# Two-layer decoder trunk: the pool of the shared tiles begins 128 bytes further on, and a rotation's scratch moves into spare columns

## The chip, the core and the metric

The kernel runs on one core of one Trainium2 chip. The metric is the device time of one execution in microseconds (us), the median of three runs. Everything is float32, or float32 split into two float32r parts, so that TensorE multiplies at its fast rate and the result keeps more digits.

## What is computed

The reference is a decoder trunk of two layers over 1024 positions of width 1024:

```python
mem_n = rmsnorm(mem, mem_norm_g)
for i in range(2):
    hn = rmsnorm(x, attn_norm_g[i])
    mix, q_cross = mla_mixer(...) if i % 2 == 0 else swa_mixer(...)
    cross = memory_cross_attention(q_cross, mem_n, w_mem_kv[i])
    x = x + concat([mix, cross]) @ w_o[i]
    a = relu(rmsnorm(x, mlp_norm_g[i]) @ w_up[i])
    x = x + (a * a) @ w_down[i]
return rmsnorm(x, final_norm_g)
```

Layer 0 mixes with latent attention of 12 heads (a low-rank projection of 928 columns: 384 for queries, 256 for keys and values, 32 for one rotary key shared by the heads, 256 for cross-attention queries). Layer 1 mixes with a sliding window of 128. In both, 4 heads attend to a memory of 256 positions. The MLP is 1024 to 4096 and back.

## The kernel before, in words

**Split products.** A product of two float32 matrices is three matmuls: high x high, high x low, low x high. `split` (L99, L100) makes the parts: ScalarE copies the value into float32r, VectorE subtracts. `mm3` (L108 to L110) and `mm3w` (L117 to L120) issue the triples, as do the up projection (L1402 to L1404) and the down projection (L1705 to L1707). Most matmuls are 128x128 weights by 512 columns.

**Stages.** Memory projections for both layers (to 36 us in the trace); layer 0's input projection (`a_in`, 43 to 141 us); its value, cross-attention, key and query work (to 245 us); the twelve heads (to 453 us); the output projection (`wo_phase`, to 558 us); the MLP's up phase (`mlp`, 558 to 873 us) and down phase (`Down`, to 1184 us). Then layer 1: input projection (`feat_mm`, to 1347 us), window attention (to 1429 us), output projection (to 1523 us), up (to 1837 us), down (to 2151 us).

**The up and down projections** use Strassen's scheme: seven products of half-size blocks in place of eight. In the up phase each of the seven right operands X[1] to X[7] stays in SBUF. X[1] and X[2] lie in the shared tiles q0 and q1, X[6] and X[5] in f0 and f1 (`open_x`, `wo_phase`); X[3], X[4] and X[7] lie in tiles of the right-hand pools. They are the moving operands, and the weights (128 columns of w_up or of sums of its blocks) come from right-hand tiles. Each product of one block of weights is twelve matmuls: four tiles of depth by the three terms. There are 16 blocks in a layer. In the down phase both operands of nearly all matmuls are right-hand tiles; the last eight steps of layer 1 take their moving operand from q0 and q1.

**Pools and addresses.** SBUF is filled from two sides. On the left side stand, in this order, `const` (constants, masks, gains, sine and cosine, `padl`), `quad`, and above it whatever the stage needs: `pa` (layer 0's input weights), `kvp` (values), `hb` (heads 0, 3, 6, 9), later `kv1p`, `qcp`, `q1p`. On the right side stand `padr` and the pools `xq`, `pm`, `cp`, `wu`, `hb1` (the other heads), `at`, `xnp`, `ws`, `rest`, `ores`. `quad` holds the large shared tiles: f0, f1, q0, q1 of 16 KB a partition each and two raw tiles of 4 KB, which change their use from stage to stage. In the profile they appear under the names of their uses: fa, fb, wm, xhls, qc, kq, woq, xnh, wf, mqf (f0 and f1 in the MLP), mqq (q0 and q1 in the MLP), wor, wsr, mr.

In the built kernel `const` begins at byte 16512 of a partition and ends at 19456, which is 76 x 256. So `quad` begins on a multiple of 256 bytes, and so do its tiles, their rows of 2 KB, and the tiles of `pa`, `kvp`, `hb`, `kv1p`, `qcp` and `q1p`. The right-hand pools `rest`, `ws`, `xnp`, `hb1`, `cp` and `wu` begin 128 bytes past a multiple of 256, `pm` 192 bytes past one. A row of `pa` is 3712 bytes, so its slices alternate between a multiple of 256 and 128 past one.

**The rotation.** `rope` (L298) rotates a row of heads: four VectorE products (L307 to L310), two of them into scratch tiles a and b, then a subtraction and an addition on POOL (L311, L312). It is called for one head of 32 columns in `a_in` (L619, eight times, scratch 64 bytes each with two buffers, from `pa`) and for twelve heads in `q_rope` (eight times, scratch from `wu2`). `a_in` writes its result to f1[:, t % 2, 0:928]; columns 928 to 1023 of those rows are not used then.

**Order.** The order of instructions on each engine follows the program text, with a scheduler of the tile framework that may move neighbouring work where it sees an engine waiting. DMAs of the large tiles go through SP's queue.

Of the kernel before, what the change touches and what calls it, by code (L numbers as in the profile page):

```python
# [9 lines left out]
F32 = mybir.dt.float32  # L10
# [9 lines left out]
P = 128  # L20
# [10 lines left out]
MLA_IN = 928  # L31
# [24 lines left out]
def trunk(  # L56
# [12 lines left out]
    def pool(name, side="left", space=None, bufs=1):  # L69
        kw = {"reuse_waits": "tile"}  # L70
        if space is not None:
            kw["space"] = space
        return tc.alloc_tile_pool(name=name, bufs=bufs, side=side, **kw)

    const = pool("const")
# [3 lines left out]
    def ps2(name):  # L79
        return psum[0].tile([P, 1024], F32, tag="s", bufs=2, name=name)  # L80
# [31 lines left out]
    def mm3w(pss, terms):  # L112

        n = len(terms)
        for i, (ah, al, bs) in enumerate(terms):
            for ps, (bh, bl) in zip(pss, bs):
                nc.tensor.matmul(ps, ah, bh, start=i == 0, stop=False)  # L117
                nc.tensor.matmul(ps, ah, bl, start=False, stop=False)
            for ps, (bh, bl) in zip(pss, bs):
                nc.tensor.matmul(ps, al, bh, start=False, stop=i == n - 1)  # L120
# [51 lines left out]
    def rstd_of(pl, src_parts, junk):  # L172

        k = len(src_parts)
        small_ct[0] += 1
        ss = pl.tile([P, 2], F32, tag="ss", bufs=4, name=f"ss{small_ct[0]}")
        z = pl.tile([P, 2], F32, tag="zs", bufs=4, name=f"zs{small_ct[0]}")
        for i, (ap, n) in enumerate(src_parts):
            nc.scalar.activation(junk[:, :n], ap, AF.Square, accum_out=ss[:, i : i + 1])
            nc.vector.tensor_scalar(z[:, i : i + 1], ss[:, i : i + 1], 1.0 / n, EPS, ALU.mult, ALU.add)  # L180
        return newton(pl, ss, z[:, :k], k)
# [38 lines left out]
    cosb = const.tile([P, NT, 16], F32, name="cosb")  # L220
    sinb = const.tile([P, NT, 16], F32, name="sinb")

    padl = const.tile([P, 16], F32, name="padl")
    padr_p = pool("padr", "right")
    padr = padr_p.tile([P, 24], F32, name="padr")
    nc.gpsimd.memset(padl, 0.0)
# [68 lines left out]

    rope_ct = [0]

    def rope(pl, src, dst, t, nh):  # L298

        rope_ct[0] += 1  # L300
        c = cosb[:, t : t + 1, :].to_broadcast([P, nh, 16])
        s = sinb[:, t : t + 1, :].to_broadcast([P, nh, 16])
        a = pl.tile([P, nh, 16], F32, tag="ra", bufs=2, name=f"ra{rope_ct[0]}")
        b = pl.tile([P, nh, 16], F32, tag="rb", bufs=2, name=f"rb{rope_ct[0]}")
        x1, x2 = src[:, :, 0:16], src[:, :, 16:32]
        V = nc.vector
        V.tensor_tensor(dst[:, :, 0:16], x1, c, ALU.mult)  # L307
        V.tensor_tensor(a, x2, s, ALU.mult)
        V.tensor_tensor(dst[:, :, 16:32], x1, s, ALU.mult)
        V.tensor_tensor(b, x2, c, ALU.mult)  # L310
        nc.gpsimd.tensor_tensor(dst[:, :, 0:16], dst[:, :, 0:16], a, ALU.subtract)  # L311
        nc.gpsimd.tensor_tensor(dst[:, :, 16:32], dst[:, :, 16:32], b, ALU.add)  # L312
# [179 lines left out]
    def quad_tile(tag, name, dt=F32):  # L492
        return quad.tile([P, 4, S], dt, tag=tag, bufs=1, name=name)
# [4 lines left out]
    fa0, f1 = quad_tile("f0", "fa0"), quad_tile("f1", "fa1")  # L498
# [26 lines left out]
    pa = pool("pa")  # L525
# [82 lines left out]
    CQC, CKR = 640, 896  # L608
    def a_in(t):
        xh, xl = xT.pop(t)  # L610
        ps = ps2(f"psin{t}")
        mm3w([ps[:, 0:512], ps[:, 512:MLA_IN]],
             [(xh[:, kt, :], xl[:, kt, :], [(wih[:, kt, 0:512], wil[:, kt, 0:512]), (wih[:, kt, 512:MLA_IN], wil[:, kt, 512:MLA_IN])]) for kt in range(KT)])
        c = f1[:, t % 2, 0:MLA_IN]
        rs = rstd_of(pa, [(ps[:, 0:QR], QR), (ps[:, QR : QR + KVR], KVR)], c)
        nc.vector.tensor_scalar(c[:, 0:QR], ps[:, 0:QR], rs[:, 0:1], None, ALU.mult)
        nc.vector.tensor_scalar(c[:, QR : QR + KVR], ps[:, QR : QR + KVR], rs[:, 1:2], None, ALU.mult)
        nc.scalar.activation(c[:, CQC : CQC + 256], ps[:, 672:928], AF.Copy, scale=0.125)
        rope(pa, ps[:, 640:672].rearrange("p (h c) -> p h c", h=1), c[:, CKR : CKR + 32].rearrange("p (h c) -> p h c", h=1), t, 1)  # L619
        cs_[t] = c  # L620

    def a_cT(t):
# [13 lines left out]
    for k in range(NT + 2):  # L636
        if 0 < k < NT:
            a_T(k)
        if 0 < k < NT - 1:
            a_N(k + 1)  # L640
        if 1 <= k <= NT:
            a_in(k - 1)
        if 3 <= k <= NT:
            next(loading, None)
        if 2 <= k <= NT:
            a_cT(k - 2)
# [157 lines left out]
    for j in range(6):  # L804
# [4 lines left out]
        ps = ps2(f"pskn{j}")  # L809
# [18 lines left out]
    def q_rope(t):  # L828
        sl = slice(t * P, (t + 1) * P)
        pq = ps1(f"psqr{t}")[:, 0:384]  # L830
        mm3(pq, [(cTh[:, kt, sl], cTl[:, kt, sl], *wqr[kt]) for kt in range(3)])
        qts[t] = f1[:, (t // 2) % 2, (t % 2) * 512 : (t % 2) * 512 + 384]
        rope(wu2, pq.rearrange("p (h c) -> p h c", h=H), qts[t].rearrange("p (h c) -> p h c", h=H), t, H)
# [100 lines left out]
    def values(h, G, k, late):  # L934

        vh, vl = vbufs[h % 2]
        c0 = 512 - width(G, k)
        order = [b[1] for b in blocks_of(h) if b[0] == G]
        first, last = k == order[0], k == order[-1]
        mms = []  # L940

        def mm(o, a, b, **kw):
            mms.append(lambda: nc.tensor.matmul(o, a, b, skip_group_check=True, **kw))  # L943

        if first and not late:
            po_[(h, G)] = ps1(f"pso{h}_{G}")
        po = po_[(h, G)]
        if (G, k) in WHOLE:
            if late:
                return [], lambda: None  # L950
            mm(po[:, c0:], vfs[h % 2][:, k, :], probs.pop((h, G, k))[:, c0:], start=first, stop=last)
        elif late:
            mm(po[:, c0:], vh[:, k, :], probs.pop((h, G, k, "late"))[:, c0:], start=False, stop=last)
        else:
            ph, probs[(h, G, k, "late")] = probs.pop((h, G, k))
            mm(po[:, c0:], vh[:, k, :], ph[:, c0:], start=first, stop=False)
            mm(po[0:64, c0:], vl[:, k, :], ph[:, c0:], start=False, stop=False)
            last = False

        def then():  # L960
            if not last:
                return
            r = slice((h % 2) * 64, (h % 2) * 64 + 64)
            if h == H - 1:
                if G:
                    last_o(G, at.tile([64, 512], F32, tag="on", bufs=2, name="rq1"))
                return
            on = at.tile([65, 512], F32, tag="on", bufs=2, name=f"on{h}_{G}")
            nc.scalar.activation(on, po[0:65], AF.Copy)
            nc.sync.dma_start(out=qn[h // 2][r, G * 512 : (G + 1) * 512], in_=on[0:64])  # L970
            c = [c for c in range(3) if h >= GRP[c]][-1]
            d0 = (h - GRP[c]) * NT + 4 * G
            nc.sync.dma_start(out=den[c][d0 : d0 + 4, :], in_=on[64:65])

        return mms, then
# [59 lines left out]
    for n in range(len(seq) + LB):  # L1035
# [3 lines left out]
        for lag, late in ((LB, True), (LV, False)):  # L1039
            if 0 <= n - lag < len(seq):  # L1040
                a, b = values(*seq[n - lag], late)
# [16 lines left out]
        h, j = divmod(n, NB)  # L1058
# [788 lines left out]
    f1 = quad_tile("f1", "fb1")  # L1847
# [230 lines left out]
```

## Time and profile before

| | |
|---|---|
| median of 3 runs | 2145.2 us (2143.55 to 2147.43) |
| profiled execution, first to last instruction | 2151.4 us, 28963 instructions |
| mean granted TensorE clock | 0.994 |
| longest single wait of TensorE (at the end of the heads) | 5.6 us |
| DMA | 286.84 MB, mean 133 GB/s |
| HBM | 183.01 MB read, 76.85 MB written |

The page gives no time for the profiled execution other than its span. In the rows of the profile, `out<-in` names the written tile and then the read ones without their buffer numbers; for a matmul the first after the arrow is the moving operand, the second the weights. "x112 | 44.2, 395 | 0.0" are count, total busy us, mean ns of one, and idle us of the engine just before. A matmul's duration is longer than the step from one to the next, since they are pipelined; the end is modelled.

### The profile page before, as it was taken

To read this page: it belongs to the slowest core of one execution; us is meant where nothing else is said; L and a number is where in the kernel's file an instruction comes from. 1 tells how busy PE (TensorE), PEld (TensorE's weight loads), DVE (VectorE), ACT (ScalarE), POOL (GpSimd) and SP (SyncE) were. 2 spreads that over 40 slices of the span, in tenths; PEclk is the share of its full clock that TensorE was granted. 3 is DMA by queue.
4 is the path that set the end of the run, shared out by engine and by line. 5 is a ranking of instruction groups with operands and counts; after the bars stand their busy time and mean duration, and the time that the engine had idled before them with its cause. 6 is when DMAs were issued, how large, how long until landed. Compare 5 with 4: busy or idle time off the path is not lost.

```text
span 2151.4 us, 28963 instructions
## 1 busy us (share of the span) xinstructions
PE 2113.6 (98%) x9830; PEld 1697.7 (79%) x9830; DVE 1473.3 (68%) x2915; ACT 1106.6 (51%) x2406; POOL 148.9 (7%) x251
## 2 busy tenths in 40 slices
PE   7999999989999999999999999999999999999998
PEld 6888766668888788888888878668888888788886
DVE  7767677764987677886557632776987766876665
ACT  6555466655754543444445432866844453444453
POOL 1001001010000000000001121530000000000000
PEclk9999999999999999999999999999999999999999
DMA  6202223333354445954433534132354446954432
GB/s 225 84 1 71 54 67 92 94 114 103 103 174 144 138 162 190 326 179 147 146 115 108 152 79 118 40 128 84 103 181 142 140 149 212 321 167 142 133 119 87
DMA packets 176436, 286.84 MB, mean 133 GB/s; under 512 B 16627, under 2 KB 68448, under 8 KB 176288
## 3 DMA queue, kind: packets, MB, share of 16 engines
q1 hardware_dynamic: 169648, 266.30, 39.1%
q0 software_dynamic: 5328, 16.07, 2.1%
q10 hardware_dynamic: 1312, 2.63, 0.4%
q8 instruction: 77, 1.26, 0.2%
q14 instruction: 71, 0.58, 0.1%
HBM read 183.01 MB, written 76.85 MB: 121 GB/s over the span
## 4 chain that ended last, share of the span: by engine, by line
PE 90%; DVE 4%; DMA 3%; ACT 2%; issue 1%; POOL 0%; SPq 0%; DVEq 0%; ACTq 0%; POOLq 0%
PE psy L1705 5%; PE psy L1707 5%; PE psy L1706 5%; PE psu L1402 5%; PE psu L1404 5%; PE psu L1403 5%; PE psz L1705 4%; PE psz L1707 4%; PE psz L1706 4%; PE psv L1404 4%; PE psv L1403 4%; PE psv L1402 4%; PE pso L943 3%; PE pss L913 3%; PE pswo L110 3%; PE pswo L108 3%
## 5 line engine op out<-in xcount | busy, mean ns | idle before, releaser
L1302 ACT ACTIVATE mr<-mr,gcol 128x256 f32<-128x256 f32 (+1 forms) x160 | 67.6, 477 | 79.4 <-DMA mr<-in_mlp_w_up_dram 70.4
L923 ACT ACTIVATE p<-pss 128x512 f32<-128x512 f32 (+2 forms) x144 | 68.4, 486 | 69.3 <-DVE pss L921 52.4
L1705 PE MATMUL psy<-g 128*128 128x512 f32 x256 | 99.9, 390 | 0.0
L1706 PE MATMUL psy<-g 128*128 128x512 f32 x256 | 99.6, 389 | 0.0
L1707 PE MATMUL psy<-g 128*128 128x512 f32 x256 | 99.4, 390 | 0.0
L99 ACT ACTIVATE g<-i 128x512 fp32r<-128x512 f32 x79 | 49.7, 629 | 93.5 <-PE psz L1706 46.3
L1302 ACT ACTIVATE d<-d,gcol 128x256 f32<-128x256 f32 x128 | 57.6, 500 | 75.2 <-DMA d<-in_mlp_w_up_dram 61.4
L100 DVE TENSOR_TENSOR g<-i,g 128x512 fp32r<-128x512 f32 x79 | 55.5, 703 | 47.8 <-ACT g L99 47.8
L99 ACT ACTIVATE i<-mr 128x512 fp32r<-128x512 f32 x78 | 49.1, 630 | 73.7 <-PE psy L1706 26.1
L943 PE MATMUL pso<-p,vf 128*128 128x512 f32 (+2 forms) x192 | 85.4, 527 | 0.5 <-ACT p L923 0.5
L792 DVE TENSOR_REDUCE m<-psx 128x1 f32<-128x1024 f32 (+7 forms) x96 | 71.9, 752 | 20.0 <-PE psx L791 19.6
L99 ACT ACTIVATE uh<-i 128x512 fp32r<-128x512 f32 x66 | 41.7, 631 | 84.6 <-PE psy L1706 39.3
L100 DVE TENSOR_TENSOR uh<-i,uh 128x512 fp32r<-128x512 f32 x66 | 45.5, 689 | 46.2 <-ACT uh L99 46.2
L1705 PE MATMUL psz<-g 128*128 128x512 f32 x192 | 74.7, 389 | 0.0
L1706 PE MATMUL psz<-g 128*128 128x512 f32 x192 | 74.7, 389 | 0.0
L1707 PE MATMUL psz<-g 128*128 128x512 f32 x192 | 74.7, 389 | 0.0
L100 DVE TENSOR_TENSOR i<-mr,i 128x512 fp32r<-128x512 f32 x78 | 53.5, 686 | 21.5 <-ACT i L99 21.5
L913 PE MATMUL pss<-qh,kh 97*128 97x512 f32 (+2 forms) x144 | 68.0, 474 | 0.0
L1618 DVE TENSOR_TENSOR mqf<-mqq,mqf 128x512 f32<-128x512 f32 x64 | 43.3, 686 | 22.1 <-DMA mqq<-in_mlp_w_down_dram 21.9
L913 PE MATMUL pss<-ql,kh 97*128 97x512 f32 (+2 forms) x144 | 58.2, 404 | 0.0
L1707 PEld LDWEIGHTS psy<-g 128*128 128x128 f32 x256 | 48.1, 188 | 10.1
L1706 PEld LDWEIGHTS psy<-g 128*128 128x128 f32 x256 | 48.1, 188 | 9.9
(655 smaller groups left out, 6890.5 us busy)
## 6 DMA issues: line engine op xcount, KB each, us to landing
i<-hd SPq DMA_DIRECT2D x154, 256.0 KB
hd<-uh SPq DMA_DIRECT2D x76, 256.0 KB
hd<-ul SPq DMA_DIRECT2D x76, 256.0 KB
mr<-in_mlp_w_up_dram SPq DMA_DIRECT2D x36, 512.0 KB
hd<-x SPq DMA_DIRECT2D x72, 256.0 KB
mr<-hd SPq DMA_DIRECT2D x70, 256.0 KB
d<-in_mlp_w_up_dram SPq DMA_DIRECT2D x32, 512.0 KB
mqq<-in_mlp_w_down_dram SPq DMA_DIRECT2D x32, 512.0 KB
```

What stands on the lines that cost most here:

```text
L99: nc.scalar.activation(hi, src, AF.Copy)
L100: nc.vector.tensor_tensor(lo, src, f32(hi), ALU.subtract)
L792: nc.vector.reduce_max(m8s[h][:, i : i + 1], ps[:, :n], axis=AX, negate=True)
L913: return lambda: nc.tensor.matmul(o, a, b, skip_group_check=True, **kw)
L943: mms.append(lambda: nc.tensor.matmul(o, a, b, skip_group_check=True, **kw))
L1302: nc.scalar.activation(w[:, k, :], w[:, k, :], AF.Copy, scale=g_mlp[layer][:, k0 + k : k0 + k + 1])
L1402: nc.tensor.matmul(ps, wh[:, k, :], xh[:, k, :], start=p in (1, 2, 5) and k == 0, stop=False, skip_group_check=True)
L1403: nc.tensor.matmul(ps, wh[:, k, :], xl[:, k, :], start=False, stop=False, skip_group_check=True)
L1404: nc.tensor.matmul(ps, wl[:, k, :], xh[:, k, :], start=False, stop=k == 3, skip_group_check=True)
L1705: nc.tensor.matmul(ps, ah[:, j, :], bh, start=p in (1, 5, 2) and k == 0, stop=False, skip_group_check=True)
L1706: nc.tensor.matmul(ps, ah[:, j, :], bl, start=False, stop=False, skip_group_check=True)
L1707: nc.tensor.matmul(ps, al[:, j, :], bh, start=False, stop=k == NP - 1, skip_group_check=True)
```

## The change

`padl` grows from 16 to 48 floats a partition, 64 to 192 bytes. `const` then ends at 19584, and `quad` and all left-hand pools above it begin 128 bytes later: 128 past a multiple of 256. The right-hand pools stay where they are. The scratch of the one-head rotation, 4 x 64 bytes of `pa`, is no longer allocated; two slices of 16 columns of f1 behind the row that the call writes take its place, alternating with t % 2 as the row does. The twelve-head rotation keeps its own scratch. The columns of `padl` that are read are the same.

```diff
-    padl = const.tile([P, 16], F32, name="padl")
+    padl = const.tile([P, 48], F32, name="padl")
...
-    def rope(pl, src, dst, t, nh):
+    def rope(pl, src, dst, t, nh, ab=None):
...
-        a = pl.tile([P, nh, 16], F32, tag="ra", bufs=2, name=f"ra{rope_ct[0]}")
-        b = pl.tile([P, nh, 16], F32, tag="rb", bufs=2, name=f"rb{rope_ct[0]}")
+        if ab is None:
+            ab = [pl.tile([P, nh, 16], F32, tag=f"r{e}", bufs=2, name=f"r{e}{rope_ct[0]}") for e in "ab"]
+        a, b = ab
...
-        rope(pa, ps[:, 640:672].rearrange("p (h c) -> p h c", h=1), c[:, CKR : CKR + 32].rearrange("p (h c) -> p h c", h=1), t, 1)
+        rope(pa, ps[:, 640:672].rearrange("p (h c) -> p h c", h=1), c[:, CKR : CKR + 32].rearrange("p (h c) -> p h c", h=1), t, 1,
+             [f1[:, t % 2, MLA_IN + 16 * i : MLA_IN + 16 * i + 16].rearrange("p (h c) -> p h c", h=1) for i in range(2)])
```

## The prediction

> **What bounds the kernel now.** I read the page's first table and its chain first, then busy time by stage, then the matmul groups, then two short stretches of the timeline.
>
> ```profile
> PE 2113.6 (98%) x9830; PEld 1697.7 (79%) x9830; DVE 1473.3 (68%) x2915; ACT 1106.6 (51%) x2406; POOL 148.9 (7%) x251
> ...
> PE 90%; DVE 4%; DMA 3%; ACT 2%; issue 1%; POOL 0%; SPq 0%; DVEq 0%; ACTq 0%; POOLq 0%
> ```
>
> TensorE is busy for 98% of the span and is 90% of the chain that ended last. By stage (start:end, length, then each engine's busy us and instruction count, granted clock, DMA share, GB/s):
>
> ```profile
> 558.00:873.00 315.00, 313.56 (x1366) 254.05 (x1365) 233.89 (x379) 160.20 (x324) 2.43 (x2) 1.00 0.49 162
> ...
> 1184.00:1347.00 163.00, 161.41 (x814) 131.41 (x812) 62.36 (x126) 55.07 (x139) 32.12 (x53) 1.00 0.45 115
> ...
> 1429.00:1474.00 45.00, 45.00 (x194) 35.77 (x192) 23.35 (x31) 28.67 (x62) 3.85 (x7) 1.00 0.54 176
> ...
> 1523.00:1837.00 314.00, 313.69 (x1363) 253.37 (x1362) 232.94 (x377) 160.47 (x324) 0.54 (x1) 1.00 0.49 164
> ```
>
> These are the two MLP up phases, layer 1's input projection and the first half of layer 1's output projection. TensorE's busy time is 99% to 100% of each, at granted clock 1.00, while VectorE has a quarter or more to spare. There the time is the number of matmuls times the step from one to the next, and only something that changes that step, or makes TensorE wait, is seen in the total.
>
> The change adds no arithmetic. It moves addresses, so the question is whether any step depends on an address. The up phase answers with matmuls of one shape (128x128 weights, 512 columns, the same three lines) whose moving operand lies in different pools (the first name after the arrow is the moving operand, the second the weights):
>
> ```profile
> L1402 PE MATMUL psu<-mqf,x 128*128 128x512 f32 x112 | 44.3, 396 | 0.4 <-ACT d L1441 0.4
> L1402 PE MATMUL psv<-mqq,i 128*128 128x512 f32 x112 | 44.2, 395 | 0.0
> ...
> L1402 PE MATMUL psu<-x,d 128*128 128x512 f32 x128 | 50.0, 391 | 0.1
> L1402 PE MATMUL psv<-g,d 128*128 128x512 f32 x112 | 43.6, 389 | 0.0
> ```
>
> mqf and mqq are the shared tiles of the pool that moves: today every 2 KB row of theirs begins at a multiple of 256 bytes. g, x, d and i are in the right-hand pools, 128 bytes past such a multiple. The first pair takes 395 to 396 ns each, the second 389 to 391 ns. The timeline gives the step itself, over twelve matmuls of one product (start, duration):
>
> ```profile
> 602.86 0.40 PE L1402 MATMUL psv<-mqq,i 128*128 128x512 f32 x1
> 603.10 0.39 PE L1403 MATMUL psv<-mqq,i 128*128 128x512 f32 x1
> 603.33 0.40 PE L1404 MATMUL psv<-mqq,i 128*128 128x512 f32 x1
> ...
> 605.66 0.40 PE L1402 MATMUL psu<-mqf,x 128*128 128x512 f32 x1
> ```
> ```profile
> 614.00 0.39 PE L1402 MATMUL psv<-g,d 128*128 128x512 f32 x1
> ...
> 616.72 0.39 PE L1402 MATMUL psu<-x,d 128*128 128x512 f32 x1
> ```
>
> 605.66 - 602.86 = 2.80 us against 616.72 - 614.00 = 2.72 us: 233 ns against 227 ns a step. No wait lies between them; in the first stretch durations alternate between 0.40 and 0.39 and the steps between 0.24 and 0.23. So TensorE pays 0.08 us for each product of twelve that streams from a shared tile.
>
> **Why I take the address for the cause.** Besides the MLP's right-hand pools (128 past 256), two other sets of tiles give this shape in 389 ns by the median (min/median/max ns): layer 0's key projection, 128 past, and the memory projection, 192 past.
>
> ```profile
> L117 PE MATMUL pskn<-cTh,wknh x24: 387/389/477, 174.6 to 200.6; 128*128 128x512 f32 x24
> ```
> ```profile
> L341 PE MATMUL psmk<-wmh,memTh x32: 387/389/628, 11.0 to 36.2; 128*128 128x512 f32 x32
> ```
>
> What reads a shared tile, as moving operand or as weights, is slower. Layer 1's projection shows both roles, with wf and without:
>
> ```profile
> L108 PE MATMUL psf<-xnh,wf x96: 397/397/450, 1278.2 to 1346.0; 128*128 128x512 f32 x96
> ...
> L109 PE MATMUL psf<-x,wf x96: 392/395/397, 1278.4 to 1346.2; 128*128 128x512 f32 x96
> ...
> L110 PE MATMUL psf<-xnh,wf x96: 388/392/402, 1278.6 to 1346.5; 128*128 128x512 f32 x96
> ```
> ```profile
> L108 PE MATMUL psf<-xnh,wsh 128*128 128x512 f32 x96 | 38.4, 400 | 0.0
> ...
> L110 PE MATMUL psf<-xnh,wsl 128*128 128x512 f32 x96 | 37.6, 391 | 0.0
> L109 PE MATMUL psf<-x,wsh 128*128 128x512 f32 x96 | 37.3, 388 | 0.0
> ```
>
> x,wsh has neither operand in the pool: 388 ns. x,wf is the same matmul with its weights in a shared tile: 395. With the pad of 192 bytes all shared tiles start 128 past a multiple of 256, as the fast ones do. I expect their matmuls to take the fast step.
>
> **The change part by part.**
>
> 1. *Up phases.* Products 1, 2, 5 and 6 of the seven stream from shared tiles: 4 x 16 blocks x 2 layers = 128 products of twelve, 128 x 0.08 = 10.2 us by the timeline. By the durations, 1536 matmuls x 6 ns = 9.2 us. I take 10.0.
>
> 2. *First halves of the two output projections*, where woq streams:
>
> ```profile
> L108 PE MATMUL pswo<-woq,x x64: 392/398/765, 453.7 to 508.9; 128*128 128x512 f32 x64
> ...
> L108 PE MATMUL pswo<-woq,d x60: 392/395/398, 1432.5 to 1473.8; 128*128 128x512 f32 x60
> ```
>
> 2 layers x 8 blocks of rows x 8 tiles of depth x 3 = 384 matmuls at 395 to 398 against 389: 384 x 6 = 2.3 us. A part of layer 0's runs at a reduced clock; I leave that out.
>
> 3. *Layer 1's projection.* Against the 388 of x,wsh: wf groups 96 x (9 + 7 + 4) ns = 1.9 us; of the ws groups I count 96 x (5 + 3) = 0.8 us, since L108's mean of 400 holds some long first steps. Together 2.7 us.
>
> 4. *End of the last down projection.* Its last eight steps stream from shared tiles too:
>
> ```profile
> L1706 PE MATMUL psy<-mqq,x 128*128 128x512 f32 x32 | 12.6, 395 | 0.0
> L1705 PE MATMUL psy<-g 128*128 128x512 f32 x16 | 6.2, 389 | 0.0
> ```
>
> 96 x 6 = 0.6 us.
>
> 5. *Layer 0's input projection* (psin, 384 matmuls): its weights xhls come off the boundary, its moving slices step by 3712 bytes, so as many land on a boundary as leave one. Its nearest price is the 7 ns of x,wf over x,wsh; bounds -0.5 us (more on a boundary) and 2.7 us (384 x 7) gain. I take 0: half of its moving reads are no better off, and its durations are mixed with throttled ones.
>
> 6. *Head, value, key and SWA tiles* move too. Heads 3 and 4 are the same code on tiles of a moved pool (on the boundary) and of an unmoved one (128 past):
>
> ```profile
> 298.50:315.90 17.40, 12.20 (x36) 6.44 (x36) 1.00 0.28 61
> 315.90:333.40 17.50, 12.21 (x36) 6.47 (x37) 1.00 0.27 62
> ```
>
> 12.20 us against 12.21 for 36 score matmuls: nothing to gain. This row also speaks against me, since the boundary costs nothing there. Those matmuls use 97 rows and are slow in both; I read it as another limit, and keep it for the first rival.
>
> 7. *VectorE and ScalarE* read the moved tiles at the same speed as others:
>
> ```profile
> L100 DVE TENSOR_TENSOR g<-mqf,g 128x512 fp32r<-128x512 f32 x64 | 43.8, 684 | 1.3 <-ACT g L99 1.3
> ...
> L100 DVE TENSOR_TENSOR i<-d,i 128x512 fp32r<-128x512 f32 x44 | 29.9, 684 | 0.4 <-ACT i L99 0.4
> ```
>
> 684 ns both: 0.
>
> 8. *The rotation's scratch.* Same six instructions per tile of tokens, writing into spare columns of f1. It has two places in turn as before (bufs=2, now t % 2), so the scratch's write after read distance is unchanged. In the built program TensorE, VectorE and ScalarE have the same work; the order differs only around the last tile's transposes, the value matmuls and the first cross-attention blocks (about 141 to 186 us). TensorE's waits there come to
>
> ```profile
> PE pscx L408 <- DVE rb L310: 0.9, 1, 0.9
> PE pscT L420 <- ACT qc L371: 0.9, 1, 0.9
> ```
>
> so a better order gains at most 1.8 us, and a worse one may cost a wait of that size twice. The built order puts the last transposes, which wait for POOL's rotation, ahead of a block of score matmuls: behind them on TensorE's queue stand the next value matmuls, and who waits for those is ScalarE's and VectorE's copying of them. I take 0, with -1.8 to +1.8.
>
> Sum: 10.0 + 2.3 + 2.7 + 0.6 = 15.6 us. The steps are on the path, but a faster TensorE comes earlier to its loads and to VectorE's splits (DMA and VectorE are 7% of the chain), so I pass on nine tenths: 14.0 us. The profiled execution's span is 2151.4 us, 6.2 above the median of the runs; I take the difference from the median: 2145.2 - 14 = **2131 us**. TensorE stays the bound; next late are the weight loads at the starts of phases.
>
> **Rivals.**
>
> *A. Not the alignment: no change.* The shared tiles may be slow for where they lie, or for a conflict that goes with them. For it: the heads' row. Against it: x,wf and x,wsh differ in the weights' tile alone, in a stage with the same traffic. Time 2145, within 2143 to 2148. [...]
>
> *B. The new offset is worse: slower.* The alternating 0.40 and 0.39 looks like every second step meeting the weight read. If what matters is the distance between the two streams and 128 past meets it in each step, the fast steps of the pair are lost. The first stretch has steps of 0.24 and 0.23 us in turn; all at 0.24 is 0.007 us more than the 0.233 mean. On the 2208 matmuls of steps 1 to 4 (1536 + 384 + 192 + 96) that is 15 us: 2160. It decides as soon as moving and weight reads, 256 apart now in place of 128, collide. Against it: groups where both operands are off the boundary are fast in all cases that the trace has.
>
> *C. Loads into the shared tiles get dearer*, their rows no longer starting on a boundary. ScalarE's waits for the up phase's loads, one set into shared tiles and one into right-hand ones:
>
> ```profile
> L1302 ACT ACTIVATE d<-d,gcol 128x256 f32<-128x256 f32 x128 | 57.6, 500 | 75.2 <-DMA d<-in_mlp_w_up_dram 61.4 <-DVE x L1466 7.1 <-DVE uh L1466 3.5
> L1302 ACT ACTIVATE mr<-mr,gcol 128x256 f32<-128x256 f32 x128 | 57.2, 499 | 75.6 <-DMA mr<-in_mlp_w_up_dram 66.6 <-DVE uh L1466 3.6 <-DVE ul L1466 3.6
> ```
>
> 61.4 us off the boundary and 66.6 on it: no penalty seen. DMA holds 3% of the chain, 65 us; a tenth more is 6.5 us, which would leave 2138. [...]
>
> **How the numbers follow.** Accuracy of a measurement here: about 0.2%, 4.3 us; less can't be told from no change. Forecast 0.68, between 2126 (15.6 and the 2.7 of psin passed on whole, and a run's spread) and 2137 (half of the steps' gain). C or another partial gain 0.08 (2137 to 2141), A 0.16, B 0.08. The range 2126 to 2146 takes in the forecast, C and most of A, and leaves B out. Faster: 0.68 + 0.07 = 0.75; same 0.17; slower 0.08.
>
> **What would show it.** Right: mqf, mqq, woq and wf groups at 389 ns like g,d, and 2.72 us for twelve steps; each up phase about 5 us shorter. Rival A: they stay at 395. Rival B: they go to 398 or more. C: longer waits on mr and mqq loads, with fast steps. The forecast is wrong if the steps are fast and the phases don't shorten (then loads or splits bind), or if the heads' matmuls get slower.

## The result and the profile after

| | before | after |
|---|---|---|
| median of 8 runs each, same chip | 2145.62 us (2142.95 to 2149.52) | 2140.82 us (2137.83 to 2144.23) |
| ratio after/before, 95% interval | | 0.9975 [0.9966, 0.9985] |
| profiled execution, span | 2151.4 us | 2139.4 us |
| granted TensorE clock in that execution | 0.994 | 0.996 |

Faster, and by more than chance, but 4.8 us and not 14. The profiled execution of before took longer than each of its eight runs, so the 12 us between the two spans are not the change's alone. From here on, lines after the rotation have moved by two: the up phase's matmuls are L1404 to L1406, ScalarE's copy-out L1443, the scaling of the weights L1304, the load L1327, the write of a hidden value L1438.

**The steps came out as forecast.** The groups of the up phase in the profile after (count, total busy us, mean ns of one, idle us just before):

```profile
L1404 PE MATMUL psu<-mqf,x 128*128 128x512 f32 x112 | 44.0, 393 | 0.0
...
L1405 PE MATMUL psv<-mqq,i 128*128 128x512 f32 x112 | 43.6, 389 | 0.0
...
L1405 PE MATMUL psv<-g,d 128*128 128x512 f32 x112 | 43.6, 389 | 0.0
...
L109 PE MATMUL psf<-x,wf 128*128 128x512 f32 x96 | 37.3, 389 | 0.0
```

mqq and wf take 389 ns where they took 395. The timeline of one product that streams from mqf (start, duration), to the first matmul of the next product:

```profile
676.37 0.39 PE L1404 MATMUL psu<-mqf,x 128*128 128x512 f32 x1
...
679.09 0.39 PE L1404 MATMUL psv<-mqf,x 128*128 128x512 f32 x1
```

679.09 - 676.37 = 2.72 us for twelve, the fast value of the prediction.

**The up phases did not get shorter.** Stage times, from the first matmul of a stage to the first of the next (us, profiled executions; e1 is the scratch change alone, with the slow steps, see below):

| stage | before | e1 | after |
|---|---|---|---|
| layer 0 output projection, first half | 55.9 | 54.2 | 53.7 |
| layer 0 up | 314.2 | 312.6 | 313.1 |
| layer 0 down | 311.6 | 311.6 | 311.5 |
| layer 1 projection | 155.4 | 155.4 | 153.3 |
| layer 1 output projection, first half | 44.9 | 44.9 | 43.7 |
| layer 1 up | 312.4 | 312.8 | 312.5 |
| layer 1 down | 314.3 | 314.0 | 313.7 |

Two stages ran at another granted clock, so their differences are not the change's alone: layer 0's input projection (98.7 and 96.3) at 0.97 before and at 1.00 after, and the first half of layer 0's output projection at 0.96 and 1.00. The columns for 43 to 140 us and 465 to 510 us (granted clock in the third column from the right), before and then after:

```profile
43.00:140.00 97.00, 94.58 (x489) 84.67 (x488) 65.26 (x258) 48.30 (x141) 2.81 (x14) 0.97 0.18 61
465.00:510.00 45.00, 45.00 (x186) 36.06 (x185) 26.37 (x34) 24.73 (x55) 3.81 (x7) 0.96 0.36 117
```
```profile
43.00:140.00 97.00, 94.36 (x506) 85.12 (x505) 66.02 (x265) 49.11 (x148) 4.66 (x16) 1.00 0.16 57
465.00:510.00 45.00, 45.00 (x201) 37.24 (x200) 24.64 (x33) 24.81 (x58) 4.91 (x9) 1.00 0.36 117
```

In the kernels below that have the slow steps, and the loads and the scaling on their old engines, layer 0's up phase takes 312.5 to 314.4 us, so 313.1 is no gain. What is left is layer 1's projection (2.1), its output projection (1.2), the last down phase (0.6) and a part of layer 0's output projection: with 192 of its matmuls 6 ns faster, 1.2 us. Sum 5.1, against 4.8 measured. The up phases, of which 10 of 15.6 us were expected, gave nothing.

**Where the 10 us went.** The chain of work that ended last, by engine, was 90% PE and 3% DMA. After the change:

```profile
PE 77%; DMA 8%; DVE 7%; ACT 5%; issue 3%; SPq 0%; POOL 0%; DVEq 0%; ACTq 0%; POOLq 0%
```

Other things than TensorE now end last for 23% of the time, where it was 10%. Product 7 of each block (psu<-g,i) shows the place. Its first line before the change, then after:

```profile
L1402 PE MATMUL psu<-g,i 128*128 128x512 f32 x120 | 47.5, 396 | 0.2 <-ACT i L1441 0.2
```
```profile
L1404 PE MATMUL psu<-g,i 128*128 128x512 f32 x120 | 49.5, 412 | 3.8 <-ACT d L1443 1.7 <-ACT i L1443 1.6
```

The idle time went from 0.2 to 3.8 us, and the mean from 396 to 412 ns. The idle time understates the stall, since the durations grew as well. In starts the steps into the first matmul of product 7 and out of it exceed 227 ns by 4.9 us (3.72 + 1.21, in 11 blocks) in layer 0 and by 4.6 us (3.44 + 1.20, in 11) in layer 1: together 9.6 us. By the same count it is 1.2 us in the kernel before, so 8.4 us of stalls are new, most of what the faster steps had brought.

The releaser is L1443, ScalarE's copy of product 6 out of PSUM. Product 7 adds into the PSUM tile of product 6 (psu), from which this copy reads, and waits for it (0.33 us at 682.30 below). Why the copy is late is seen on ScalarE's timeline, in one block (idle before and its releaser in brackets):

```profile
672.28 0.91 ACT L1304 ACTIVATE mr<-mr,gcol 128x256 f32<-128x256 f32 x2 [3.46 <-DMA mr<-in_mlp_w_up_dram]
673.10 0.58 ACT L1447 ACTIVATE uh<-psu 128x512 f32<-128x512 f32 x1
673.57 0.62 ACT L99 ACTIVATE d<-mr 128x512 fp32r<-128x512 f32 x1
...
680.34 0.91 ACT L1304 ACTIVATE mr<-mr,gcol 128x256 f32<-128x256 f32 x2 [3.36 <-DMA mr<-in_mlp_w_up_dram]
681.16 0.61 ACT L99 ACTIVATE x<-d 128x512 fp32r<-128x512 f32 x1
681.68 0.57 ACT L1443 ACTIVATE i<-psu 128x512 f32<-128x512 f32 x1
```

and on TensorE's and SP's:

```profile
681.59 0.39 PE L1406 MATMUL psv<-mqf,x 128*128 128x512 f32 x1
682.30 0.50 PE L1404 MATMUL psu<-g,i 128*128 128x512 f32 x1 [0.33 <-ACT i L1443]
```
```profile
667.83 0.38 SPq L1327 DMA_DIRECT2D mr<-in_mlp_w_up_dram  x1
...
672.39 3.56 SPq L1438 DMA_DIRECT2D hd<-uh  x3
676.04 0.57 SPq L1327 DMA_DIRECT2D mr<-in_mlp_w_up_dram  x1
```

Product 6 ended at about 679.3 (its last matmul started at 678.87 and took 0.39). Its copy could have run then. But ScalarE took its instructions in the order of its queue, and at 676.98 it had come to the scaling of the weights of the block after next. The load of their second half was issued at 676.04 and landed at 680.3; until then ScalarE stood, 3.36 us, and only then came a split and the copy (681.68). Product 7 began at 682.30 and not at 681.82. It is a loop: as I read the order, the load could not be issued much earlier, because its tile was freed by the split L99 at 673.57 (and VectorE's half of it), with one more write ahead on SP's queue; and that split stood on ScalarE behind the scaling of the first half, which had waited 3.46 us for the load of 667.83. ScalarE's total idle time ahead of the scaling of mr grew from 75.6 us to

```profile
L1304 ACT ACTIVATE mr<-mr,gcol 128x256 f32<-128x256 f32 x128 | 57.1, 499 | 84.2 <-DMA mr<-in_mlp_w_up_dram 76.8 <-DVE x L1468 3.8 <-DVE uh L1468 3.6
```

From the first matmul of product 7 of one block to that of the next, the mean over both layers is 19.44 us before and 19.45 us after (26 of these stretches in each). The faster steps alone would give 84 x 0.2267 = 19.04 us, and the slow ones alone 19.37 us (e6 below). So the kernel before was already stopped now and then by what stops the changed one: its block took 0.08 us more than its steps.

### The profile page after: what moved, and what is told of

Its sections match the earlier page's. It is cut to its first block, busy times and chain, and to the rows that moved or that the text cites. A ratio compares the mean times of both kernels' runs of the same rounds, so it can differ in the third digit from the quotient of the medians.

```text
span 2139.4 us, 28961 instructions
## 1 busy us (share of the span) xinstructions
PE 2099.5 (98%) x9830; PEld 1693.2 (79%) x9830; DVE 1473.1 (69%) x2915; ACT 1106.5 (52%) x2406; POOL 149.9 (7%) x251
## 4 chain that ended last, share of the span: by engine, by line
PE 77%; DMA 8%; DVE 7%; ACT 5%; issue 3%; SPq 0%; POOL 0%; DVEq 0%; ACTq 0%; POOLq 0%
PE psy L1707 5%; PE psy L1709 5%; PE psy L1708 5%; PE psz L1707 4%; PE psz L1709 4%; PE psz L1708 4%; PE psu L1404 3%; DMA mr<-in_mlp_w_up_dram 3%; PE psu L1406 3%; PE psu L1405 3%; PE pso L945 3%; PE pss L915 3%; DMA d<-in_mlp_w_up_dram 3%; PE pswo L110 3%; PE pswo L108 3%
## 5 line engine op out<-in xcount | busy, mean ns | idle before, releaser
L1304 ACT ACTIVATE mr<-mr,gcol 128x256 f32<-128x256 f32 (+1 forms) x160 | 67.4, 477 | 88.3 <-DMA mr<-in_mlp_w_up_dram 80.8
L1304 ACT ACTIVATE d<-d,gcol 128x256 f32<-128x256 f32 x128 | 57.6, 500 | 78.6 <-DMA d<-in_mlp_w_up_dram 64.1
L99 ACT ACTIVATE g<-i 128x512 fp32r<-128x512 f32 x79 | 49.7, 629 | 92.9 <-PE psz L1708 46.0
L99 ACT ACTIVATE uh<-i 128x512 fp32r<-128x512 f32 x66 | 41.7, 632 | 84.5 <-PE psy L1708 39.7
L99 ACT ACTIVATE i<-mr 128x512 fp32r<-128x512 f32 x78 | 49.1, 630 | 68.2 <-PE psy L1708 25.6
```

The source lines that it names most:

```text
L99: nc.scalar.activation(hi, src, AF.Copy)
L1304: nc.scalar.activation(w[:, k, :], w[:, k, :], AF.Copy, scale=g_mlp[layer][:, k0 + k : k0 + k + 1])
```

## Experiments

The theory: the change makes the steps as fast as forecast, but in the up phases TensorE comes up against a second bound that lay right beside the first, the wait of ScalarE's queue for the next block's load. Rivals: a part of the gain is the scratch's; the fast step isn't what the prediction took it for; or ScalarE's and VectorE's work, the loads' traffic, or the loop's own length hold the phase.

### Which part of the change, and which addresses (e1 to e4, e9, e10)

These six kernels differ from the changed kernel in the pads alone; TensorE's and VectorE's orders are the same. e1 has the old pad, and so only the scratch in the spare columns is new in it.

```diff
-    padl = const.tile([P, 48], F32, name="padl")
+    padl = const.tile([P, 16], F32, name="padl")
```

> The scratch change alone, with the old pad of 64 bytes (shared tiles on a multiple of 256 again). Theory (the whole gain is the pad's): 2145.5 us, ratio 1.000 within 0.001; the twelve steps of psv<-mqq,i take 2.80 us and the duration is 395 to 396 ns again. Rival (part of the 4.8 us comes from the rotation's scratch and the order around it): 2141 to 2143, with the slow steps.

Measured: 2147.73 us, ratio to before 1.0001 [0.9992, 1.0010]. mqq takes 395 ns again, and the mean block 19.43 us. The scratch and the order around it are worth nothing that can be told; the gain is the pad's.

The same line with 32 columns (e2), 64 (e3) and 80 (e4):

> The pad is 128 bytes, so that the shared tiles begin 64 bytes past a multiple of 256. Alignment theory in its narrow form (a row that begins on a multiple of 256 is the slow one): fast steps, 227 ns, 389 ns a matmul, time as with the pad of 192, 2141. Distance theory (what counts is that moving operand and weights start the same number of bytes past 256, or 128 apart): other steps than 227, for the weights and the right-hand moving tiles stay 128 past. Location theory: any move is enough, 227.

> The pad is 256 bytes, so that the shared tiles begin 192 bytes past a multiple of 256. Alignment theory in its narrow form: 227 ns a step, about 2141. Distance theory: the same as with 64 past, since weights at 128 past are 64 away on the other side. The memory projection, 192 past in the kernel before, took 389 ns, which speaks for 227.

> The pad is 320 bytes, so that the shared tiles lie 256 bytes later than before, on a multiple of 256 once more. Alignment theory: the slow steps return (2.80 us for twelve, 395 to 396 ns), and the time with them, 2145.5. Rival (the old place itself was bad, any other is good): 2.72 us, 2141.

| kernel | shared tiles, bytes past 256 | right-hand pools, bytes past 256 | mean step of mqq and mqf, ns | us | ratio to before |
|---|---|---|---|---|---|
| before | 0 | 128 | 233 | | |
| e1 | 0 | 128 | | 2147.73 | 1.0001 [0.9992, 1.0010] |
| e2 | 64 | 128 | 233 | 2149.90 | 1.0013 [1.0004, 1.0021] |
| after | 128 | 128 | 227 | 2140.82 | 0.9975 [0.9966, 0.9985] |
| e3 | 192 | 128 | 229 (231, 226, 229) | 2146.10 | 0.9997 [0.9987, 1.0006] |
| e4 | 0 (256 bytes later) | 128 | | 2146.71 | 1.0000 [0.9991, 1.0008] |
| e9 | 0 | 0 | 227 | 2141.50 | 0.9975 [0.9965, 0.9985] |
| e10 | 64 | 64 | 227 | 2143.48 | 0.9989 [0.9980, 0.9997] |

(Steps are from start to start; the three of e3 are its three lines L1404 to L1406. For e1 and e4 the durations are given: psv<-mqq,i takes 395 ns in both, as before.) The rows of e2, e3 and e4:

```profile
L1405 PE MATMUL psv<-mqq,i 128*128 128x512 f32 x112 | 44.1, 394 | 0.0
```
```profile
L1404 PE MATMUL psv<-mqq,i 128*128 128x512 f32 x112 | 44.1, 394 | 0.0
...
L1406 PE MATMUL psv<-mqq,i 128*128 128x512 f32 x112 | 43.9, 392 | 0.0
...
L1405 PE MATMUL psv<-mqq,i 128*128 128x512 f32 x112 | 43.5, 388 | 0.0
```
```profile
L1405 PE MATMUL psv<-mqq,i 128*128 128x512 f32 x112 | 44.2, 395 | 0.0
```

The place (e4) is not the cause, but neither is a row's start on a multiple of 256 as such: 64 past is as slow (e2, 233 ns), and 192 past is slow in two of the three lines (e3, 231 and 229). The narrow form's 2141 us missed in both. The mean steps up to here fit one rule: all three lines are fast (227 ns, in the changed kernel) when the moving operand and the weights stand the same number of bytes past a multiple of 256. That was tested by moving the right-hand pools as well (the edit of e9; e10 has 32 and 40 columns):

```diff
-    padl = const.tile([P, 48], F32, name="padl")
+    padl = const.tile([P, 16], F32, name="padl")
...
-    padr = padr_p.tile([P, 24], F32, name="padr")
+    padr = padr_p.tile([P, 56], F32, name="padr")
```

> The changed kernel with the left pad at 64 bytes again and the right-hand pad 128 bytes larger: shared tiles and right-hand pools now all begin on a multiple of 256 bytes (the right-hand pools are 128 bytes lower than before). Same order on every engine. Phase theory, formed on the pads of 128 and 256 bytes (a step is fast when the moving operand and the weights stand the same number of bytes past a multiple of 256, wherever that is): psv<-mqq,i and psv<-g,d both at 227 ns, 389 ns, time as the changed kernel, 2140 to 2142. Narrow alignment theory of the prediction (a row that begins on a multiple of 256 is slow by itself): everything goes to 233 ns, psv<-g,d and the down phases too, some 6900 long matmuls x 6 ns = 41 us over the changed kernel, 2180.

> As the last, with shared tiles and right-hand pools 64 bytes past a multiple of 256 (left pad 128 bytes, right-hand pad 64 larger). Phase theory: 227 ns in all groups, 2140 to 2142. Absolute theory (64 past is a bad place, as the pad of 128 bytes might also mean): psv<-g,d goes to 233 ns, 2160 or more.

With everything on a multiple of 256 (e9) no step is slow, neither in the shared tiles nor in the right-hand ones (390 ns in both rows):

```profile
L1404 PE MATMUL psu<-g,i 128*128 128x512 f32 x120 | 49.4, 412 | 3.3 <-ACT i L1443 1.4 <-ACT d L1443 1.3
...
L1405 PE MATMUL psv<-mqq,i 128*128 128x512 f32 x112 | 43.6, 390 | 0.0
L1405 PE MATMUL psv<-g,d 128*128 128x512 f32 x112 | 43.6, 390 | 0.0
```

The time is the changed kernel's, 0.9975, and the stall ahead of product 7 is there too (412 ns, 3.3 us idle). e10 has the same steps (psv<-mqq,i and psv<-g,d take 390 ns); its 2143.48 us is over the 2140 to 2142 that were expected, but its ratio, 0.9989 [0.9980, 0.9997], overlaps that of the changed kernel. So in these kernels the step goes with where the two operands stand to each other, not with the place of one: 227 ns with both at 0, 64 or 128. Why the step is shorter there was not tried, nor whether it is a matmul's own weights that count or those of the next one, which lie in the same tiles.

### What holds the up phases (e5, e6)

The loads of blocks 4 to 15 are left out; the instructions on what lies in the tiles are the same. TensorE's order is too, but the framework's scheduler wrote other orders for ScalarE and VectorE in both kernels, so what these runs show of the loads includes that.

```diff
         def load_raw(i):
+            if i >= 4:
+                raws[i] = keep[i % 2]
+                return
             r = [m.raw() for _ in range(2)] if i % 2 == 0 else [m.t(f"d{j}") for j in range(2)]
-            raws[i] = r = [...]
+            keep[i % 2] = raws[i] = r = [...]
```

> The changed kernel, in which the up phases load w_up for blocks 0 to 3 alone; blocks 4 to 15 scale, add and split what lies in the two pairs of raw tiles (24 of 32 blocks without their loads, all engines with the same instructions). Theory (the gain was lost because TensorE now waits, through ScalarE's queue, for the loads of the next block): the stall of 0.45 us ahead of product 7 goes, each up phase is about 5 us shorter (308 in place of 313), the time about 2131 to 2132. Rival 1 (ScalarE or VectorE themselves have no more time per block): no change, 2141, the stalls stay. Rival 2 (the loads' traffic slows the matmuls' operand reads): the step itself gets shorter than 227 ns.

> The kernel before with the same loads left out. Theory: there TensorE with its 233 ns a step is the slower of the two, so the loads hide: at most 1 us is gained, 2144.5 to 2145.5. Rival 1: no change either. Rival 2 (loads cost both kernels the same): as much as in the changed kernel, some 10 us, 2136.

Changed kernel without the loads: 2130.24 us, 0.9930 [0.9917, 0.9942], up phases 307.5 and 306.7. Kernel before without them: 2145.32, 0.9996 [0.9987, 1.0005], up phases 312.6 and 311.3. The same loads cost the changed kernel some 10 us (2140.82 to 2130.24 by the medians, 0.0045 by the ratios) and the kernel before nothing that can be told. The stall is gone, and the mean step is what it was:

```profile
L1407 PE MATMUL psu<-g,i 128*128 128x512 f32 x120 | 46.7, 389 | 0.0
...
L1409 PE MATMUL psv<-mqq,i 128*128 128x512 f32 x112 | 43.6, 389 | 0.0
```

From block to block it is 19.04 us against 19.37 in e6. Rival 1 falls (ScalarE and VectorE do the same work in 19.04 us, if in another order), and rival 2 (the matmul takes 389 ns with the loads and without).

### Two moves that failed (e7, e8, e11, e12)

Loads on POOL's queue:

```diff
-                nc.sync.dma_start(out=r[h], in_=wsrc[...])
+                (nc.sync if i < 2 else nc.gpsimd).dma_start(out=r[h], in_=wsrc[...])
```

> The changed kernel, the loads of w_up for blocks 2 to 15 issued on POOL's queue, which stands empty in the phase, in place of SP's, where they stand behind the writes of the hidden values. Theory: the second half of a load starts about 1 us earlier (676.04 in the trace against a tile that is free at 675.0), twice what TensorE waits for, so most of the stall goes: each up phase 3 to 5 us shorter, 2131 to 2135. Rival 1 (engine work, not loads): 2141. Rival 3 (the transfer itself, 4.2 us, and the freeing of the tile decide, and the place in the queue doesn't): 2139 to 2141.

> The kernel before with its loads on POOL's queue. Theory: nothing to gain, 2145 to 2146, since TensorE's own steps set the time there. Rival 3: nothing either. If it gains as much as the changed kernel does, the loads bound both kernels and the theory falls.

Measured: 2180.64 (1.0162 [1.0148, 1.0176]) and 2183.31 (1.0171 [1.0157, 1.0185]). Both forecasts missed. TensorE's order stayed, but with another queue for the loads the framework's scheduler wrote another order for ScalarE and VectorE as well. In layer 0's up phase ScalarE's waits for the loads grew from 72 us in the changed kernel to 83 us, and what stands behind them waits longer: VectorE's sums in d for the scaling 20.5 us against 5.4, TensorE's weight loads for the copies into d 13.3 against 4.2 (e7, 560 to 892 us: engine, line, waited for, us, times, longest):

```profile
ACT d L1304 <- DMA d<-in_mlp_w_up_dram: 44.7, 13, 5.0
...
DVE d L1343 <- ACT d L1304: 20.5, 5, 5.2
...
PEld psu L1404 <- ACT d L1443: 13.3, 8, 3.0
```

The median block takes 20.8 us (e7) and 20.7 us (e8): with the loop longer, the fast and the slow step give the same up phases (335.2 and 334.5 us in layer 0, 329.7 and 328.4 in layer 1).

The scaling of the second half on POOL, loads as they were:

```diff
             for h in range(2):
+                if h == 1 and i >= 2:
+                    w = raws[i][1]
+                    for k in range(4):
+                        nc.gpsimd.tensor_scalar(w[:, k, :], w[:, k, :], g_mlp[layer][:, 4 + k : 5 + k], None, ALU.mult)
+                    continue
                 scale_w(layer, raws[i][h], 4 * h)
```

> The changed kernel; in the up phases the scaling of the second half of each block's weights (blocks 2 to 15, four instructions of 128x256) is done by POOL and not by ScalarE. The loads stay on SP's queue. Theory (ScalarE's in-order queue, standing at the second half's scaling until its load lands, holds up the copy that product 7 waits for): ScalarE's copies no longer stand behind that load; the 0.45 us a block goes or gets much smaller, each up phase 3 to 5 us shorter, 2131 to 2135. Rival (the loop load, scale, split, free tile, load is itself too long, whoever scales): POOL's four instructions take longer than ScalarE's, so no gain, or a loss: 2141 to 2146.

> The kernel before with the same move of the second half's scaling to POOL. Theory: TensorE's steps set the time there, so nothing is gained, 2145 to 2146. If it gains several us, the loads held up the kernel before as well.

Measured: 2187.81 (1.0195 [1.0180, 1.0210]) and 2192.98 (1.0220 [1.0205, 1.0234]). The rival's direction, but far more than it said. POOL takes 0.93 us for each of the four in mr and 0.98 us in d (0.5 on ScalarE), and the wait moved to VectorE, whose sums now stand in its queue until POOL is done (e11, 560 to 892 us):

```profile
DVE i L1348 <- POOL mr L1336: 36.5, 7, 6.1
...
DVE d L1348 <- POOL d L1336: 33.7, 6, 6.0
```

Neither move separates "the loop is too long" from "the scaling stands at the wrong place in the queue", since both changed the orders too.

### The place in the queue alone (e13 to e15)

The scaling stays on ScalarE; it is only told behind which copy it stands. TensorE's order stays that of the kernel changed by it. The scheduler answered on VectorE too: in e13 and e14 a split of each block moved up past one or two of the sums, in e15 more moved. The edit shown is that of e13 and e14 (first half behind the copy of product 1 of the block two before, second half behind that of product 6); in e15 both halves stand behind the copy of product 5.

```diff
             for h in range(2):
-                scale_w(layer, raws[i][h], 4 * h)
+                with tc.issue_after(ev[(i - 2, (1, 6)[h])]) if i >= 2 else nullcontext():
+                    scale_w(layer, raws[i][h], 4 * h)
...
-                nc.scalar.activation(s, ps, AF.Copy)
+                ev[(i, p)] = nc.scalar.activation(s, ps, AF.Copy).ins
```

> The changed kernel with an order given to ScalarE in the up phases: the scaling of the first half of a block's weights (blocks 2 to 15) stands behind the copy-out of product 1 of the block two before it, that of the second half behind the copy-out of product 6. Same instructions, TensorE's order the same. Theory (it is the place of the scaling on ScalarE's in-order queue, ahead of the copies, that turns the load's landing into a wait of product 7): the 0.45 us a block goes, each up phase about 5 us shorter (308), 2130 to 2133. Rival (the loop of load, scale, sum, split and freed tile is too long in itself, wherever the scaling stands): product 7 or a later product waits just as long, 2139 to 2142.

> The kernel before with the same order on ScalarE. Theory: nothing is gained while the step is 233 ns, 2144 to 2146. Rival: the same.

> The changed kernel, with both halves' scaling behind the copy-out of product 5 (one copy later than in the last but one), so that the loads have some 4 to 10 us more to land. Theory: as that one or a little better, 2129 to 2133. Rival: 2139 to 2142, or more, as a later scaling lengthens the loop.

| | kernel before | changed kernel |
|---|---|---|
| order as it was | 1 | 0.9975 [0.9966, 0.9985] |
| scaling behind the copies (e14, e13) | 0.9991 [0.9981, 1.0002], 2145.72 us | 0.9923 [0.9907, 0.9939], 2131.04 us |
| both halves behind product 5 (e15) | | 0.9924 [0.9908, 0.9939], 2131.36 us |

The order alone gains nothing that can be told on the kernel before; on the changed kernel it gains the missing 10 us (9.8 by the medians, 0.0052 or 11 us by the ratios). That VectorE's small moves have a part in it is not ruled out, but e13 and e15 differ in them and take the same time. ScalarE's timeline in e13 (lines one or two further on):

```profile
673.83 0.58 ACT L1445 ACTIVATE i<-psu 128x512 f32<-128x512 f32 x1
674.30 1.70 ACT L1305 ACTIVATE mr<-mr,gcol 128x256 f32<-128x256 f32 x4
...
679.22 0.58 ACT L1445 ACTIVATE i<-psu 128x512 f32<-128x512 f32 x1
679.69 1.69 ACT L1305 ACTIVATE mr<-mr,gcol 128x256 f32<-128x256 f32 x4
```

The copy of product 6 runs at 679.22, behind one split and 2.2 us ahead of the start of product 7 (681.43), and the scaling behind it finds its weights there: the brackets are gone. The second half's load is issued earlier as well; as I read the order, because the split that frees its tile no longer stands behind a wait:

```profile
666.75 0.38 SPq L1328 DMA_DIRECT2D mr<-in_mlp_w_up_dram  x1
...
674.21 0.39 SPq L1328 DMA_DIRECT2D mr<-in_mlp_w_up_dram  x1
```

That is 7.46 us after the first half, where it was 8.21. ScalarE's waits for the loads and product 7's first line:

```profile
L1305 ACT ACTIVATE mr<-mr,gcol 128x256 f32<-128x256 f32 x128 | 54.9, 498 | 16.6 <-DMA mr<-in_mlp_w_up_dram 16.6
...
L1406 PE MATMUL psu<-g,i 128*128 128x512 f32 x120 | 46.8, 390 | 1.1 <-ACT i L1445 1.1
```

The wait goes from 84.2 to 16.6 us, and the mean of product 7's first line from 412 to 390 ns. The block takes 19.04 us, as without the loads, and the up phases are 309.5 and 306.7 us (307.6 and 307.0 in e15). In the chain of work from 560 us to about the end of layer 0's up phase, by line, the changed kernel and then e13:

```profile
by line: PE psu L1404 11.3%; PE psu L1406 10.5%; PE psu L1405 10.5%; DMA mr<-in_mlp_w_up_dram 9.8%; DMA d<-in_mlp_w_up_dram 9.4%; PE psv L1404 7.1%; PE psv L1405 7.1%; PE psv L1406 7.1%; issue 4.3%; ACT d L1304 2.7%; DMA mqf<-in_mlp_w_down_
```
```profile
by line: PE psu L1406 17.5%; PE psu L1408 17.4%; PE psu L1407 17.3%; PE psv L1406 13.1%; PE psv L1407 13.1%; PE psv L1408 13.0%; DMA mqf<-in_mlp_w_down_dram 2.1%; DMA mr<-in_mlp_w_up_dram 1.9%; issue 0.9%; DVE x L1437 0.4%; DVE x L1458 0.4%
```

The loads' 19% of the chain become 2%. With these stalls gone, the changed kernel stands 0.77% under the kernel before, at the 2131 us of the forecast.

## Why the prediction was wrong

The forecast was 2131 us with a range from 2126 to 2146. 2140.8 lies in the range, but the size of the gain was off by a factor of three.

1. *Up phases, 10.0 us:* **the step that failed.** "128 x 0.08" was right for the matmuls: 2.72 us for twelve, and some 10 us as soon as ScalarE's order lets TensorE have it. Wrong was that the phases would shorten by it: 8.4 us of new stalls stood in its place. The premise "there the time is the number of matmuls times the step" was read from TensorE's busy share of 99% to 100% in the two windows. It shows who is the bound, not how near the next one is. TensorE's steps took 19.37 us a block, and with ScalarE's old order the mean block takes 19.43 to 19.50 us in before, after, e1 to e4, e9 and e10, whether the steps are slow or fast. The forecast needed 0.33 us a block below 19.37, and with that order there was none to be had.
2. *First halves of the output projections, 2.3 us:* layer 1's gained 1.2, as half of this. Layer 0's steps went from 233 to 227 ns, which is 1.2 us too, but its stage time moved with the granted clock (0.96 and 1.00). Against e1, at 1.00 as well, it gained 0.5 (54.2 to 53.7).
3. *Layer 1's projection, 2.7 us:* 2.1 measured (155.4 to 153.3). The ws groups gave less than counted: the step of xnh,wsl went from 228.4 to 227.6 ns, and that of x,wsh from 226.1 up to 227.6.
4. *Last down phase, 0.6 us:* 0.6 measured, within what stages differ.
5. *Layer 0's input projection, 0:* right by the steps, whose mean is 210 ns before and after (those under 300 ns), and by e1, which has the old addresses and the same granted clock of 1.00 as the changed kernel: 95.4 and 95.5 us from the first of these matmuls to the first behind the last.
6. and 7. *Heads, VectorE, ScalarE, 0:* heads 208.8 and 209.0 us. Right.
8. *Scratch, 0:* e1, ratio 1.0001. Right.

*Nine tenths passed on.* The margin for "TensorE comes earlier to its loads" was one tenth, 1.6 us, since DMA and VectorE held 7% of the chain. A share of the chain doesn't tell the slack of what is not on it. A row that pointed to it was quoted, under rival C: ScalarE idle 75.6 us ahead of the scaling, 66.6 of it for a load. I used it to compare two sets of tiles, and did not ask what stands behind the scaling on ScalarE's queue, where the copy that product 7 waits for would have been found. The last sentence of the prediction named the outcome ("the steps are fast and the phases don't shorten") without a price or a chance of its own; "C or another partial gain" took in its time, 2137 to 2141, with 0.08, but not its reason.

*Rival A (not the alignment)* falls by the steps: they changed (233 to 227 ns), and e4 puts the old durations back (395 ns). The same instructions take 233 ns a step in e2 and 227 in e9, which differ in the two pads alone. *Rival B (the distance between the streams)* fell as a forecast, but its idea was the better one: distance counts, and 128 past was good with weights that stood there too (227 ns; in e2, with the weights still at 128 and the shared tiles at 64, 233). That the forecast step came out at 128 past was luck in this sense: "every row off the boundary is fast" would have failed at 64 (e2, 233 ns). The two sets that the prediction took as a sign for the boundary, the key and the memory projection, have both operands in pools that begin the same number of bytes past 256 (128 and 192, 389 ns by the median in both), so they speak for the distance as well. *Rival C (dearer loads)* had the right place and the wrong cause: in e9 the shared tiles start on multiples of 256 again, and the stall (412 ns, 3.3 us) and the time (0.9975) are the changed kernel's. Dearer loads aren't needed to explain it; TensorE got fast enough to wait for them.

## What to carry to other kernels

A busy share of 99% to 100%, as in the two up phases before the change, names the bound and hides the margin (8.4 us of new stalls took the place of the faster steps): before a gain per step is multiplied by a count, follow one period of the loop on each in-order queue and ask what stands behind the longest wait there. An engine's wait for data that are needed only a block later cost nothing that can be told until the work queued behind it was due: ScalarE waited 66.6 us for the loads of mr before the change, where leaving loads out gave 0.9996 (e6), and 76.8 us after it, where it gave some 10 us (e5). In the shape measured here (128x128 weights, 512 columns, float32r) a step took 227 ns with both operands the same number of bytes past a multiple of 256 (0, 64 and 128) and 229 to 233 ns on the mean of its three lines with them 64 or 128 apart: place them alike, and test a change that moves one of them with the other moved along.

## What the runs showed of the hardware that was not expected

- For a 128x128 weight and 512 columns in float32r, the step went with where moving operand and weights stand relative to each other, counted past a multiple of 256 bytes: equal 227 ns (at 0 in e9, 64 in e10 and 128 in the changed kernel), 64 apart 233 or 229 on the mean of three lines (moving operand 64 past and weights 128 past, e2, or 192 and 128, e3), 128 apart 233 (the kernel before; e4, 256 bytes further on, has its 395 ns a matmul again).
- A matmul whose own two operands had not moved got slower when its neighbours' did: psf<-x,wsh, with x and wsh in right-hand pools, took 388 ns before and 397 in e2 and in e3, and its step went from 226 ns (mean) to 236.5 and 235.4. In e2 and e3 its neighbours read shared tiles 64 and 192 past, and before on a multiple of 256; what in them makes the difference was not tried. e2's row:

```profile
L109 PE MATMUL psf<-x,wsh 128*128 128x512 f32 x96 | 38.1, 397 | 0.0
```

- A scaling of 128x256 float32 took 0.93 to 0.98 us on POOL (e11) against 0.50 us on ScalarE (the changed kernel).
